# Scores of the first 128 tokens as one unsplit product, from a copy that ScalarE writes

## The chip, the cores and the metric

The kernel runs on one core of a Trainium2 chip. The metric is the device time of one execution in microseconds; the times given are medians of runs. TensorE (PE in the profile) multiplies, VectorE (DVE), ScalarE (ACT) and GpSimd (POOL) work on elements, and SyncE (SP) issues most transfers. Each engine has its own queue and works through it in order; semaphores make one wait for another.

## The reference

Two layers over 512 tokens of width 1024, all in fp32. Each layer has three attention branches with sigmoid gates and an MLP:

```python
for l in range(DEPTH):
    h = _rms_norm(x, attn_norm[l])
    proj = h @ w_in[l]
    ...
    o_a = _dilated_mixture(aq, ak, ...)                 # branch A
    bq = jnp.einsum('bsr,rhe->bshe', _rms_norm(b_ql, ...), w_q_b[l])
    ...                                                 # bk likewise; norms, rotary part
    o_b = _causal_softmax_attention(bq, bk, bv)         # branch B: 8 heads, 96 wide
    o_c = _stick_breaking_attention(c_q, c_k, c_v)      # branch C
    merged = gates[0] * (o_a @ ...) + gates[1] * (o_b @ ...) + gates[2] * (o_c @ ...)
    x = x + merged @ w_out[l]
    h2 = _rms_norm(x, mlp_norm[l])
    x = x + jnp.square(jax.nn.relu(h2 @ w_ff1[l])) @ w_ff2[l]
```

The change is in branch B, for its first block of 128 query tokens (t = 0): `s = q @ k.T * 96**-0.5` under a causal mask, then softmax.

## The kernel before

Activations are kept transposed, 128 rows of the feature axis by 512 tokens. Nearly every product is split: an operand x is held as a high part rounded to float32r and a low part, the rest, and `mm3` (L338 to L340) or `denseA` (L489 to L491) issues high x high, high x low and low x high into one PSUM bank. The splits are made by `split`: ScalarE writes the high part (L346 or L349), VectorE the low part (L347 or L350). Weights are streamed by SP into `raww` and split into `hl` (L250 in the profile, a line that all operations of the weight and gate helpers share).

PSUM has eight banks: three of tag d (psd in the profile, dense products), two of s (pss, scores), two of t (pst, transposes), one of o (pso, outputs). A bank is used again only when its readers are done.

For each head of branch B, `turn` calls `to_qT` for the query and for the key: four transposes on TensorE (L570) bring 512 tokens of the 96-wide head into one bank of tag t, and `split` writes the pair `qT` with the gain column bcol as scale. `score` makes the scores of one block of 128 queries; for t = 0 only 128 keys are needed, but 256 columns are multiplied (m = max(n, 256)). Softmax follows on VectorE (L605) and ScalarE (L608, exponential), `pt_put` transposes the weights (L770, tag t again) and splits them into PP (L346, L347), `causal_out` multiplies with the values. The order within a branch is the hand-written list UNITS_B; `layer` lays it between the dense products of the list ORDER by a credit of estimated times, and a scheduler then fixes the order on each engine.

TensorE's dense products read as streamed operand either tiles of tag a4 (normed activations, trace name a) or of tag u4 (trace name u: the merged branches, read by the output projection, and the squared MLP activations, read by the down-projection). Both are 128 rows by two parts of 512 fp32. In each layer the output projection and each of the four quarters of the down-projection issue 8 tiles x 8 x 3 = 192 products with u.

At the start `warm` writes constants and issues eight products of ones (L378); `kbd_open` fills the unused halves of branch A's key tiles with zeros (L582 on POOL, L583 on VectorE or ScalarE), once in each layer. The tiles of pool kp lie one behind another in the memory, with the other pools behind them; x0, the first one of 2,112 bytes a row, is among the first.

Of the kernel before, what the change touches and what calls it, by code (L numbers as in the profile page):

```python
# [11 lines left out]
AF = mybir.ActivationFunctionType  # L12
# [4 lines left out]
P = 128  # L17
L = 2
D = 1024
S = 512  # L20
# [8 lines left out]
QK = 96  # L29
# [225 lines left out]
class Kern:  # L255
    BUFS = dict(
        raww=2, hl=3, a4=13, x2=9, gt=3, tmp=3, ot=1, sm=8, sm8=4, sm2=4, sm8b=2, u4=16,
        dg=1, raw=2, qT=2, kT=2, SN=9, PT=2, VS=1, PR=2, st=6, mx=8, PP=2, sq=2,
        qT_B=4, SN_B=4, SN_C=3, SR_C=2,
    )  # L260

    PB = dict(d=3, s=2, t=2, o=1)
# [104 lines left out]
    def warm(self, k):  # L367

        nc = self.nc
        self.zero = k([P, 1], "zero")  # L370
        nc.gpsimd.memset(self.zero, 0.0)
        self.ones = k([P, P], "ones")
        nc.vector.memset(self.ones, 1.0)
        self.onesr = k([P, P], "onesr", F32R)
        nc.vector.tensor_copy(self.onesr, self.ones)
        ps = self.ps("o")
        for i in range(self.nwarm):
            nc.tensor.matmul(ps[:, :P], self.ones, self.ones, start=True, stop=True)  # L378

    def setup(self, es):  # L380
        tc, nc = self.tc, self.nc
        self.cp = es.enter_context(tc.tile_pool(name="cp", bufs=1))
        self.kp = es.enter_context(tc.tile_pool(name="kp", bufs=1))
        self.pp = es.enter_context(tc.tile_pool(name="pp", bufs=2, space=PSUM))
        self.wsetup()
        self.x = []
        k = lambda shape, nm, dt=F32: self.kp.tile(shape, dt, name=nm, tag=nm)
        self.bcol = k([96, L, 2], "bcol")
        self.warm(k)
        x0 = k([P, 2 * KT + S], "x0")[:, : KT + S]  # L390
        self.cut = KT + S // 2
        for c in (slice(0, self.cut), slice(self.cut, KT + S)):
            nc.scalar.dma_start(x0[:, c], self.ins["x0g"][:, c])
        nc.scalar.add_instruction(
            mybir.InstLoadActFuncSet(name=nc.get_next_instruction_name(), act_func_set_id=ACT_SET, ins=[], outs=[])
        )
        self.gain0 = x0[:, :KT]
        self.x.append(x0[:, KT:])
        self.wload(1)
        for j in range(1, KT):  # L400
            xt = self.t(self.cp, "x2", [P, S])
            nc.sync.dma_start(xt, self.ins["xT"][j])
            self.x.append(xt)
            if j == 1:
                self.wload(2)
        self.gain = k([P, L, NG], "gain")
        nc.sync.dma_start(self.gain, self.ins["gain"])
        self.ident = k([P, P], "ident")
        self.ropes = k([P, NROPE], "ropes")
        self.masks = k([P, NMASK], "masks", BF16)  # L410
        self.maskA = self.masks[:, C_MA : C_MA + 256]
        self.maskR = self.masks[:, C_MR : C_MR + 256]
        self.maskB = self.masks[:, C_MB : C_MB + 512]
        self.resetC = self.masks[:, C_MC : C_MC + 512]

    def tables(self):

        nc = self.nc
        with self.tc.issue_after(self.wdma[4].ins):
            nc.sync.dma_start(self.ident, self.ins["ident"])  # L420
            nc.sync.dma_start(self.ropes, self.ins["ropes"])
            nc.sync.dma_start(self.masks, self.ins["masks"])
        nc.gpsimd.dma_start(self.bcol, self.ins["bcol"])


    def norm_begin(self, goff, l):
# [135 lines left out]
        nc.gpsimd.tensor_tensor(t, src, grow.unsqueeze(1).to_broadcast([P, 4, 2 * w]), ALU.mult)  # L562
        return t[:, :, 0:w], t[:, :, w : 2 * w]

    def to_qT(self, y, g, d=P):

        nc = self.nc
        ps = self.ps("t")
        for t in range(NT):
            nc.tensor.transpose(ps[:d, t * P : t * P + P], y[:, t], self.ident)  # L570
        hl = self.t(self.tp, "qT", [P, 2, S], F32R)
        self.split(hl[:d, 0], hl[:d, 1], ps[:d], g)
        return hl

    def kbd_open(self):

        nc = self.nc
        z = self.zero.unsqueeze(2)
        self.kbds = []
        for f in (nc.vector.tensor_copy, nc.scalar.copy):  # L580
            k = self.t(self.tp, "kT", [P, 2, 2, S], F32R)
            nc.gpsimd.tensor_copy(k[0:64, :, 1, :], z[0:64].to_broadcast([64, 2, S]))  # L582
            f(k[64:128, :, 0, :], z[64:128].to_broadcast([64, 2, S]))  # L583
            self.kbds.append(k)

    def kbd(self):
# [218 lines left out]
    def layer(self, l):  # L805
# [18 lines left out]
        def thread_A():  # L824
            with tc.tile_pool(name=f"ta{l}", bufs=1) as tp:
                self.tp, self.phase = tp, "A"
                tabs["qn"] = self.rope_tab(R_N, 8, g(21, 53), "tqn")
                tabs["kn"] = self.rope_tab(R_N, 8, g(53, 85), "tkn")
                tabs["qr"] = self.rope_tab(R_R, 8, g(21, 53), "tqr")
                tabs["kr"] = self.rope_tab(R_R, 8, g(53, 85), "tkr")  # L830
                self.kbd_open()
                yield ("open", "A")
                oA = [self.t(self.cp, "a4", [P, 2, S], F32R) for _ in range(2)]
                st["oA"] = oA
                sn, sr, qk, pt, pr, w = {}, {}, {}, {}, {}, {}
                s0 = [self.t(tp, "st", [P, 4, 4]) for _ in range(2)]
                s1 = [self.t(tp, "st", [P, 4, 4]) for _ in range(2)]

                def norm(a, tab):
                    self.head_norm(st[a], 4, HD, 0, 8, tabs[tab])  # L840
                    yield 0.0

                def turn(key, aq, ak, i):
                    pair = lambda a: st[a][:, :, 2 * i : 2 * i + 2].rearrange("p t h d -> p t (h d)")
                    q = self.to_qT(pair(aq), g(19, 20))
                    yield 0.5
                    qk[key] = q, self.to_kbd(pair(ak), g(20, 21))
                    yield 0.5

                def nat(i, t):  # L850
                    self.a_nat(*qk["n", i], i, t, s0[i], sn)
                    yield 0.65

                def res(h, r):
                    self.a_res(*qk["r", h], h, r, s1[h // 2], sr)
                    yield 0.33

                def mix(i):
                    w[i] = self.a_mix(s0[i], s1[i])
                    yield 0.0  # L860

                def scale(h):
                    self.a_scale(h, sn, sr, *w[h // 2])
                    yield 0.0

                def trn(h, half):
                    pt[h, half] = self.a_trn(h, half, sn)
                    yield 0.43

                def trr(h, half):  # L870
                    pr[h, half] = self.a_trr(h, half, sr)
                    yield 0.43

                def out(h):
                    self.a_out(h, [pt[h, 0], pt[h, 1]], [pr[h, 0], pr[h, 1]], st["vA"], st[f"vr{h // 2 + 1}"], oA[h // 2])
                    yield 2.8

                bn = b_norm(0)
                for u in UNITS_A:
                    a = u.split(":")  # L880
                    k, n = a[0], [int(x) for x in a[1:] if x.isdigit()]
                    if k in ("need", "raw"):
                        yield (k, a[1])
                    elif k == "norm":
                        yield from norm(a[1], a[1][0] + ("n" if a[1][1] == "0" else "r"))
                    elif k == "turn":
                        if a[1] == "n":
                            yield from turn(("n", n[0]), "q0", "k0", n[0])
                        else:
                            i = 1 + n[0] // 2  # L890
                            yield from turn(("r", n[0]), f"q{i}", f"k{i}", n[0] % 2)
                    elif k == "bn":
                        yield from bn_part(bn)
                    else:
                        f = dict(nat=nat, res=res, mix=mix, scale=scale, trn=trn, trr=trr, out=out)[k]
                        yield from f(*n)
            yield ("done", "A")
# [7 lines left out]
        def thread_B():  # L905
            with tc.tile_pool(name=f"tb{l}", bufs=1) as tp:
# [6 lines left out]

                def turn(h, name, d, col):
                    def f():
                        d[h] = self.to_qT(st[f"{name}{h // 4}"][:, :, h % 4], self.bcol[:, l, col : col + 1], QK)
                        yield 0.5
                        if name == "bk" and h % 4 == 3:
                            yield ("raw", "bq1" if h == 3 else "cq")
                    return f  # L920

                def score(h, t):
                    def f():
# [2 lines left out]
                        m = max(n, 256)  # L926
                        sl = slice(t * P, t * P + P)
                        q, k = qT[h], kT[h]
                        self.mm3(ps[:, :m], q[:96, 0, sl], q[:96, 1, sl], k[:96, 0, :m], k[:96, 1, :m], True, True)
                        s = self.t(tp, "SN", [P, S])  # L930
                        sm = self.small()
                        self.softmax_scores(ps[:, :n], n, s[:, :n], self.maskB[:, 512 - n :], QK ** -0.5, sm[:, 0:1], sm[:, 1:2])
# [463 lines left out]
```

## Time and profile before

| | us |
|---|---|
| median of 3 runs (1812.24 to 1812.69) | 1812.52 |
| the profiled execution | 1812.14 |
| its span (first to last instruction) | 1810.4 |
| TensorE busy in the span | 1799.3 |
| VectorE busy | 1165.3 |
| ScalarE busy | 931.0 |
| POOL busy | 37.2 |

A row of the timeline gives start, duration, engine, line, operation, out<-in, and in brackets the idle time before it and who ended it; rows of a like kind are merged with their count (x4), and the duration is then that of the whole group. A row of the groups gives line, engine, operation, shapes and count, then busy us and the mean ns of one. Durations of TensorE's products are modelled and overlap, so their spacing is read from start to start. In `128*128 128x512` the first pair is the weight tile (rows * columns), the second the streamed operand.

### The profile page before, as it was taken

How to read it: one execution, taken by the hardware profiler on the slowest of the kernel's cores; microseconds unless marked ns; L12 is line 12 of the kernel's file. 1: busy time of each engine (PE TensorE's matmuls, PEld its weight loads, DVE VectorE, ACT ScalarE, POOL GpSimd, SP SyncE). 2: the span in 40 equal slices, each digit the busy share in tenths (PEclk: the TensorE clock that was granted, in tenths of full speed). 3: DMA queues.
4: the chain of work that ended last, by engine and by line, in shares of the span. 5: the costliest groups of instructions: out<-in, count | busy, mean ns of one | idle time of the engine just before them, and what ended most of it. 6: DMA issues, size and time to landing. Idle time of an engine off the chain costs nothing.

```text
span 1810.4 us, 23064 instructions
## 1 busy us (share of the span) xinstructions
PE 1799.3 (99%) x8592; PEld 1511.7 (84%) x8592; DVE 1165.3 (64%) x2141; ACT 931.0 (51%) x1745; POOL 37.2 (2%) x66
## 2 busy tenths in 40 slices
PE   9999999999999999999999999999999999999999
PEld 8999888878888888888889988887778888888887
DVE  8666899888865343434575568997988653434342
ACT  6646677777734232323355366677877442323241
POOL 1000000000000000000010000000000000000000
PEclk9999999999999999999999999999999999999999
DMA  5222141323353222322432222413234433233332
GB/s 193 87 82 82 59 140 59 117 87 123 123 165 99 97 93 94 104 94 93 137 106 87 82 71 77 145 48 117 80 119 152 145 97 101 93 93 100 98 94 93
DMA packets 64992, 186.79 MB, mean 103 GB/s; under 512 B 11504, under 2 KB 12272, under 8 KB 64880
## 3 DMA queue, kind: packets, MB, share of 16 engines
q1 hardware_dynamic: 57888, 178.57, 30.1%
q0 software_dynamic: 1952, 6.29, 1.0%
q8 instruction: 68, 1.11, 0.2%
q10 hardware_dynamic: 5040, 0.45, 0.2%
q14 instruction: 44, 0.36, 0.1%
HBM read 168.45 MB, written 16.78 MB: 102 GB/s over the span
## 4 chain that ended last, share of the span: by engine, by line
PE 90%; DVE 7%; ACT 3%; issue 1%; DVEq 0%; ACTq 0%
PE psd L491 22%; PE psd L489 22%; PE psd L490 21%; PE psd L338 3%; PE psd L339 3%; PE psd L340 3%; PE pss L338 1%; PE pst L770 1%; DVE SN L987 1%; PE pss L339 1%; PE pss L340 1%; PE pst L570 1%; DVE hl L250 1%; PE pss L979 1%; PE pso L338 1%; PE pso L339 1%
## 5 line engine op out<-in xcount | busy, mean ns | idle before, releaser
L250 ACT CAST hl<-raww 128x1024 fp32r<-128x1024 f32 (+2 forms) x287 | 298.4, 1040 | 664.5 <-PE psd L491 485.1
L489 PE MATMUL psd<-a,hl 128*128 128x512 f32 x1232 | 484.7, 393 | 0.0
L490 PE MATMUL psd<-a,hl 128*128 128x512 f32 x1232 | 483.9, 393 | 0.0
L491 PE MATMUL psd<-a,hl 128*128 128x512 f32 x1232 | 483.6, 393 | 0.0
L250 DVE TENSOR_TENSOR hl<-raww,hl 128x1024 fp32r<-128x1024 f32 (+2 forms) x287 | 347.2, 1211 | 148.2 <-ACT hl L250 147.6
L489 PEld LDWEIGHTS psd<-a,hl 128*128 128x128 f32 x1232 | 231.7, 188 | 44.3
L491 PEld LDWEIGHTS psd<-a,hl 128*128 128x128 f32 x1232 | 231.6, 188 | 44.4
L490 PEld LDWEIGHTS psd<-a,hl 128*128 128x128 f32 x1232 | 231.7, 188 | 44.2 <-issue 0.3
L489 PE MATMUL psd<-u,hl 128*128 128x512 f32 (+1 forms) x648 | 253.6, 391 | 0.0
L491 PE MATMUL psd<-u,hl 128*128 128x512 f32 (+1 forms) x648 | 252.3, 389 | 0.0
L490 PE MATMUL psd<-u,hl 128*128 128x512 f32 (+1 forms) x648 | 249.9, 386 | 0.0
L1328 DVE TENSOR_TENSOR x<-x,psd 128x512 f32<-128x512 f32 x63 | 43.3, 688 | 188.7 <-PE psd L491 188.7
L491 PEld LDWEIGHTS psd<-u,hl 128*128 128x128 f32 x648 | 121.6, 188 | 27.9
L490 PEld LDWEIGHTS psd<-u,hl 128*128 128x128 f32 x648 | 121.6, 188 | 26.5
L1309 DVE SCALAR_TENSOR_TENSOR tmp<-psd,rrep 128x512 f32<-128x512 f32 x64 | 44.3, 692 | 151.9 <-PE psd L491 151.8
L489 PEld LDWEIGHTS psd<-u,hl 128*128 128x128 f32 x648 | 121.9, 188 | 23.7
L338 PE MATMUL psd<-hl,a 128*128 128x512 f32 (+3 forms) x328 | 121.9, 373 | 0.5 <-DVE VS L250 0.5
L339 PE MATMUL psd<-hl,a 128*128 128x512 f32 (+3 forms) x328 | 121.7, 371 | 0.0
L340 PE MATMUL psd<-hl,a 128*128 128x512 f32 (+3 forms) x328 | 121.0, 370 | 0.0
L250 ACT ACTIVATE gt<-gt 128x512 f32<-128x512 f32 x144 | 90.0, 628 | 21.8 <-DVE gt L250 18.5
L338 PEld LDWEIGHTS psd<-hl,a 128*128 128x128 f32 x328 | 79.3, 242 | 4.9 <-DVE VS L250 1.1
L339 PEld LDWEIGHTS psd<-hl,a 128*128 128x128 f32 x328 | 79.2, 241 | 4.1 <-DVE hl L250 0.6
(237 smaller groups left out, 2406.3 us busy)
## 6 DMA issues: line engine op xcount, KB each, us to landing
raww<-w SPq DMA_DIRECT2D x277, 512.0 KB, 3.5
gpark<-gt SPq DMA_DIRECT2D x48, 256.0 KB, 2.4
gt<-gpark SPq DMA_DIRECT2D x48, 256.0 KB, 3.8
x<-xT POOLq DMA_DIRECT2D x8, 256.0 KB, 4.1
park<-x POOLq DMA_DIRECT2D x8, 256.0 KB, 2.3
x<-park POOLq DMA_DIRECT2D x8, 256.0 KB, 3.9
x<-xT SPq DMA_DIRECT2D x7, 256.0 KB, 6.0
outT<-x SPq DMA_DIRECT2D x7, 256.0 KB, 2.0
```

The costliest lines, as they stand in the source:

```text
L250: return f(*a, **k)
L338: mm(ps, ah, bh, start=start, stop=False)
L339: mm(ps, ah, bl, start=False, stop=False)
L340: mm(ps, al, bh, start=False, stop=stop)
L489: self.nc.tensor.matmul(o, w[:, 0, c : c + P], t[:, 0], start=k == 0, stop=False)
L490: self.nc.tensor.matmul(o, w[:, 0, c : c + P], t[:, 1], start=False, stop=False)
L491: self.nc.tensor.matmul(o, w[:, 1, c : c + P], t[:, 0], start=False, stop=k == last)
L570: nc.tensor.transpose(ps[:d, t * P : t * P + P], y[:, t], self.ident)
L770: nc.tensor.transpose(ps[:, kt * P : kt * P + P], s[:, kt * P : kt * P + P], self.ident)
L979: nc.tensor.matmul(ps[:, :m], q[:, hh, sl], k[:, i, hh, :m], start=i == 0, stop=i == 1)
L1309: nc.vector.scalar_tensor_tensor(t, ps, 0.0, self.rrep, ALU.max, ALU.mult)
L1328: nc.vector.tensor_tensor(x, x, ps, ALU.add)
```

## The change

Four edits:

1. `to_qT` gets a further tile `full`: ScalarE writes the first 128 tokens of the transposed head, scaled, unsplit, as plain fp32 (tag q32, four buffers, 128 x 128). It does so for query and key of each head: 32 new instructions.
2. `score` at t = 0 issues one plain fp32 product of 128 columns from these copies in place of the three split ones of 256.
3. x0 is allocated with 4 KT instead of 2 KT extra columns: 2,176 bytes instead of 2,112. All tiles behind it move by 64 bytes. By the built programs the u4 tiles start at byte 152,576 of each partition instead of 152,512 (= 1191.5 x 128), in steps of 4,096; the a4 tiles start at 30,848 (= 241 x 128) in both. qT, kT, PP, SN, ident and masks move as u4 does.
4. The zero fills: POOL fills only the first of the two key tiles, VectorE the lower half of the first and the upper half of the second, ScalarE the rest; in layer 1 they are put behind the copy onesr. The load of bcol goes from POOL's queue to SP's.

```diff
-        qT_B=4, SN_B=4, SN_C=3, SR_C=2,
+        q32=4, qT_B=4, SN_B=4, SN_C=3, SR_C=2,
...
-        nc.vector.tensor_copy(self.onesr, self.ones)
+        onesr = nc.vector.tensor_copy(self.onesr, self.ones)
+        self.kz = lambda: self.tc.issue_after(onesr.ins)
...
-        x0 = k([P, 2 * KT + S], "x0")[:, : KT + S]
+        x0 = k([P, 4 * KT + S], "x0")[:, : KT + S]
...
-        nc.gpsimd.dma_start(self.bcol, self.ins["bcol"])
+        nc.sync.dma_start(self.bcol, self.ins["bcol"])
...
-    def to_qT(self, y, g, d=P):
+    def to_qT(self, y, g, d=P, full=None):
...
         self.split(hl[:d, 0], hl[:d, 1], ps[:d], g)
+        if full is not None:
+            nc.scalar.activation(full[:d], ps[:d, :P], AF.Copy, scale=g)
         return hl
...
-    def kbd_open(self):
+    def kbd_open(self, l):
...
-        for f in (nc.vector.tensor_copy, nc.scalar.copy):
+        for fs in ((nc.gpsimd.tensor_copy, nc.vector.tensor_copy), (nc.vector.tensor_copy, nc.scalar.copy)):
             k = self.t(self.tp, "kT", [P, 2, 2, S], F32R)
-            nc.gpsimd.tensor_copy(k[0:64, :, 1, :], z[0:64].to_broadcast([64, 2, S]))
-            f(k[64:128, :, 0, :], z[64:128].to_broadcast([64, 2, S]))
+            for i, f in enumerate(fs):
+                r = slice(64 * i, 64 * i + 64)
+                with self.kz() if l == 0 else ExitStack():
+                    f(k[r, :, 1 - i, :], z[r].to_broadcast([64, 2, S]))
...
-                        d[h] = self.to_qT(st[f"{name}{h // 4}"][:, :, h % 4], self.bcol[:, l, col : col + 1], QK)
+                        d[h, 0] = self.t(tp, "q32", [P, P])
+                        d[h] = self.to_qT(st[f"{name}{h // 4}"][:, :, h % 4], self.bcol[:, l, col : col + 1], QK, d[h, 0])
...
-                        self.mm3(ps[:, :m], q[:96, 0, sl], q[:96, 1, sl], k[:96, 0, :m], k[:96, 1, :m], True, True)
+                        if t == 0:
+                            nc.tensor.matmul(ps[:, :n], qT[h, 0][:96], kT[h, 0][:96], start=True, stop=True)
+                        else:
+                            self.mm3(ps[:, :m], q[:96, 0, sl], q[:96, 1, sl], k[:96, 0, :m], k[:96, 1, :m], True, True)
```

How the instructions stand on an engine, before and with the change, is shown at two places. The first is TensorE at head 0 of branch B in layer 1. Names are those of the tiles with their numbers: pss are score banks, q_372 and q_369 the new copies of key and query. Before:

```order
L338 MATMUL pss_2102<-qT_2099,qT_2091 128x256
L570 MATMUL pst_2112<-ident,raw_1768 96x128
L338 MATMUL pss_2120<-qT_2099,qT_2091 128x256
L490 MATMUL psd_2319<-a_25_156,hl_2171 128x512
L491 MATMUL psd_2319<-a_25_156,hl_2171 128x512
L489 MATMUL psd_2319<-a_27_162,hl_2171 128x512
L490 MATMUL psd_2319<-a_27_162,hl_2171 128x512
L491 MATMUL psd_2319<-a_27_162,hl_2171 128x512
L339 MATMUL pss_2102<-qT_2099,qT_2091 128x256
L340 MATMUL pss_2102<-qT_2099,qT_2091 128x256
```

With the change, the same engine and place:

```order
L571 MATMUL pst_2115<-ident,raw_1768 96x128 x4
L491 MATMUL psd_2325<-a_27_162,hl_2179 128x512
L492 MATMUL psd_2325<-a_27_162,hl_2179 128x512
L490 MATMUL psd_2325<-a_29_168,hl_2179 128x512
L491 MATMUL psd_2325<-a_29_168,hl_2179 128x512
L492 MATMUL psd_2325<-a_29_168,hl_2179 128x512
L936 MATMUL pss_2106<-q_372_2096,q_369_2086 128x128
L338 MATMUL pss_2124<-qT_2102,qT_2092 128x256
```

The three products into the bank of block 0 (pss_2102 before) have become one (L936), and the scores as a whole have moved behind more dense products.

The second place is the key of head 4 in layer 1, where the bank that the four transposes fill (pst_2779) is taken again two groups of transposes later (pst_2804). ScalarE before, from the split's high part on:

```order
L349 ACTIVATE qT_2773<-pst_2768,bcol 96x512
L346 CAST PP_2078<-pst_2776 128x3x128
L250 ACTIVATE gt_3189<-gt_3189 128x512 x2
L250 CAST hl_3325<-raww_3266 128x1024
L346 CAST PP_2078<-pst_2792 128x4x128
```

ScalarE with the change:

```order
L349 ACTIVATE qT_2784<-pst_2779,bcol 96x512
L346 CAST PP_2078<-pst_2788 128x3x128
L250 ACTIVATE gt_3205<-gt_3205 128x512 x2
L250 CAST hl_3341<-raww_3282 128x1024
L575 ACTIVATE q_532_2778<-pst_2779,bcol 96x128
```

The copy (L575) has come in behind two gate instructions and a weight cast, where before ScalarE was done with that bank after its first row. TensorE with the change, between the two uses of the bank:

```order
L571 MATMUL pst_2779<-ident,raw_2650 96x128 x4
L775 MATMUL pst_2788<-ident,SN_2485 128x128 x3
L490 MATMUL psd_3284<-a_27_162,hl_3065 128x512
...
L490 MATMUL psd_3346<-a_14_124,hl_3175 128x512
L491 MATMUL psd_3346<-a_14_124,hl_3175 128x512
L775 MATMUL pst_2804<-ident,SN_2475 128x128 x4
```

Left out are eight more dense products, so eleven stand between; before there were eight and one score product between the same groups of transposes.

More of the change, by code (lines that the diff above doesn't have):

```diff
@@ L830, in thread_A @@
                 tabs["kr"] = self.rope_tab(R_R, 8, g(53, 85), "tkr")
-                self.kbd_open()
+                self.kbd_open(l)
                 yield ("open", "A")
```

## The prediction

> **What bounds the kernel now.** I read the page first (busy shares and the chain that ended last), then the windows of the stretch in which the second branch runs, then the timeline of TensorE at the lines that change.
>
> ```profile
> span 1810.4 us, 23064 instructions
> PE 1799.3 (99%) x8592; PEld 1511.7 (84%) x8592; DVE 1165.3 (64%) x2141; ACT 931.0 (51%) x1745; POOL 37.2 (2%) x66
> ...
> PE 90%; DVE 7%; ACT 3%; issue 1%; DVEq 0%; ACTq 0%
> ```
>
> TensorE is busy for 99% and carries 90% of the chain. Its ends are modelled, so I go by starts, but the reading stands: what changes TensorE's own time, or makes it wait, arrives at the end; what VectorE and ScalarE do is free until TensorE waits for it. By stretch (columns: PE, PEld, DVE, ACT, POOL busy with counts, granted clock, DMA):
>
> ```profile
> 200.00:330.00 130.00, 129.68 (x729) 109.52 (x728) 121.54 (x303) 97.73 (x216) 6.46 (x9) 1.00 0.26 88
> ...
> 644.00:687.00 43.00, 43.00 (x191) 35.58 (x190) 19.87 (x23) 16.48 (x22) 0.00 (x0) 1.00 0.29 97
> 688.00:731.00 43.00, 43.00 (x190) 35.27 (x189) 15.63 (x17) 9.23 (x10) 0.00 (x0) 1.00 0.30 97
> ```
>
> The first row is the second branch in layer 1: VectorE is busy 121.5 of 130 us and ScalarE 97.7, so little room is left beside TensorE there. The other two are a quarter of the MLP, up- and down-projection, with both helpers mostly idle.
>
> **Part 1, the scores of the first 128 tokens.** Removed: three products of 256 columns for each of 8 heads and 2 layers. Four of them stand in a row here:
>
> ```profile
> 221.91 0.28 PE L339 MATMUL pss<-qT,qT 96*128 96x256 f32 x1
> 222.03 0.28 PE L340 MATMUL pss<-qT,qT 96*128 96x256 f32 x1
> 222.15 0.28 PE L339 MATMUL pss<-qT,qT 96*128 96x256 f32 x1
> 222.26 0.28 PE L340 MATMUL pss<-qT,qT 96*128 96x256 f32 x1
> ```
>
> From start to start (222.26 - 221.91) / 3 = 0.117 us, so three cost 0.35 us. Added: one product of plain fp32 operands, 128 columns. No such product with 96 rows is in the trace, so I bound it by the two kinds of plain fp32 products that are. Both leave two records for each product in the code (the loop at L1090 issues 4 and shows 8, the one at L751 issues 8 or, for two heads together, 16 records for 8).
>
> ```profile
> 1008.46 0.28 PE L340 MATMUL pss<-kT,qT 128*128 128x256 f32 x1
> 1008.57 0.95 PE L1090 MATMUL pso<-ones,tmp 128*128 128x1 f32 x8
> 1009.38 0.37 PE L338 MATMUL pss<-kT,qT 128*128 128x256 f32 x1
> ...
> 157.26 0.28 PE L746 MATMUL pso<-PT,VS 128*128 128x256 f32 x1
> 157.46 1.96 PE L751 MATMUL pso<-PR,x 128*64 128x128 f32 x16
> 159.35 0.38 PE L752 MATMUL pso<-PT,VS 128*128 128x256 f32 x1
> 159.58 0.28 PE L753 MATMUL pso<-PT,VS 128*128 128x256 f32 x1
> ```
>
> At L1090 the end of the split product before is 1008.74 and of the one behind 1009.75: 1.01 us for 8 records and one split product (0.117), 0.11 us a record and nothing for the change of kind. At L751, from L746's start to L753's, 2.32 us hold 16 records and two split products: with (1.96 - 0.27) / 15 = 0.113 us a record and 2 x 0.117, 0.28 us are left over for going in and out. L751 loads only 64 columns of weights (128*64); the new product loads 128 like L1090, so I take L1090: 2 x 0.11 = 0.22 us, a gain of 0.13 each, 16 x 0.13 = **-2.0 us**. The other end, with 0.28 us for each isolated pair: 16 x (0.50 - 0.35) = +2.4 us.
>
> **Part 2, ScalarE's 32 copies, and who waits for them.** The price of one comes from three rows:
>
> ```profile
> L349 ACT ACTIVATE qT<-pst,bcol 96x512 fp32r<-96x512 f32 x32 | 21.8, 680 | 8.3 <-PE pst L570 8.1
> ...
> L346 ACT CAST PP<-pst 128x512 fp32r<-128x512 f32 x32 | 18.6, 580 | 3.9 <-PE pst L770 3.6
> ...
> L346 ACT CAST PP<-pst 128x128 fp32r<-128x128 f32 x32 | 8.5, 264 | 5.0 <-PE pst L770 4.8
> ```
>
> 384 columns fewer are 580 - 264 = 316 ns less, so the scaled copy of 128 columns is about 680 - 316 = 0.36 us; 32 of them are 11.6 us of ScalarE. The copy is no matter for its length, but it reads the transposed tile in PSUM, tag t with two banks. The transposes after the next must wait until it is done, and on ScalarE it stands behind other work. This is the second place shown in the section on the change (the key of head 4), as it ran before:
>
> ```profile
> 278.05 0.61 PE L570 MATMUL pst<-ident,raw 128*96 128x128 f32 x4
> 278.50 0.49 PE L770 MATMUL pst<-ident,SN 128*128 128x128 f32 x3
> 278.70 0.69 ACT L349 ACTIVATE qT<-pst,bcol 96x512 fp32r<-96x512 f32 x1 [1.98 <-PE pst L570]
> ...
> 279.29 0.46 ACT L346 CAST PP<-pst 128x384 fp32r<-128x384 f32 x1
> ...
> 279.65 1.30 ACT L250 ACTIVATE gt<-gt 128x512 f32<-128x512 f32 x2
> 279.89 0.74 DVE L350 SCALAR_TENSOR_TENSOR qT<-pst,bcol,qT 96x512 fp32r<-96x512 f32 x1
> ...
> 280.86 1.03 ACT L250 CAST hl<-raww 128x1024 fp32r<-128x1024 f32 x1
> ...
> 281.06 0.60 PE L770 MATMUL pst<-ident,SN 128*128 128x128 f32 x4
> ```
>
> The bank that L570 filled at 278.05 is taken again by the four transposes at 281.06. Before, VectorE's L350 released it at 280.63 and nobody waited. Now the copy stands behind two sigmoids and a weight cast, so it runs from about 281.85 to 282.2. In the new order three transposes and eleven split products stand between, 3 x 0.11 + 11 x 0.23 = 2.9 us from 278.50, so TensorE arrives at 281.35 and waits about 0.9 us; in both layers 1.8 us. At the other turns I compared the same two sums by the order and these durations: four of the remaining fifteen per layer come out within 0.3 us of each other, the rest leave a microsecond or more. I add 0.5 us for those: **+2.3 us**, between 0 (ScalarE catches up elsewhere) and ten such stalls, 9 us. The new product itself also waits for both copies, but 2.5 to 20 us of other products stand between. VectorE's queue only gains from what is removed: nothing.
>
> **Part 3, the padding.** It moves every tile behind it by 64 bytes: u4 (the trace's u) from byte 152,512, which is 64 over a multiple of 128, to 152,576, which is a multiple; the a4 tiles (the trace's a) have the same shape and lie on a multiple in both. Both stream 512 columns against the same hl weights in blocks of 8 x 24 = 192 products (three lines, 64 each):
>
> ```profile
> 643.90 0.40 PE L489 MATMUL psd<-a,hl 128*128 128x512 f32 x1
> ...
> 687.47 0.40 PE L489 MATMUL psd<-u,hl 128*128 128x512 f32 x1
> ...
> 731.43 0.40 PE L489 MATMUL psd<-a,hl 128*128 128x512 f32 x1
> ...
> L489 PE MATMUL psd<-a,hl 128*128 128x512 f32 x64 | 24.9, 390 | 0.0
> ...
> L489 PE MATMUL psd<-u,hl 128*128 128x512 f32 x64 | 25.2, 394 | 0.0
> ```
>
> With a, 687.47 - 643.90 = 43.57 us; with u, 731.43 - 687.47 = 43.96 us, though the helpers do less there (windows above). There are four such blocks of u and one of the output projection in each layer: 10 x 0.39 = **-3.9 us** if the start address is the reason. The other end is 0. The same shift reaches about 180 products of 512 columns whose streamed tile lies behind u4's offset (qT, kT, PP): at the same 2 ns each 180 x 2 ns = **-0.4 us**, between 0 and -1.
>
> **Part 4, the head and the zero fills.** One of POOL's fills goes to VectorE, behind onesr, and the bcol load goes from POOL's queue to SP's, ahead of a weight load.
>
> ```profile
> 1.75 2.31 DVE L375 CAST onesr<-ones 128x128 fp32r<-128x128 f32 x1
> 4.18 0.36 DVE L439 TENSOR_SCALAR a<-x 128x256 fp32r<-128x256 f32 x1
> ...
> 4.03 0.62 ACT L250 CAST hl<-raww 128x512 fp32r<-128x512 f32 x1
> ...
> 4.70 1.22 PE L338 MATMUL psd<-hl,a 128*128 128x512 f32 x2
> ...
> 25.42 0.92 ACT L250 CAST hl<-raww 128x864 fp32r<-128x864 f32 x1 [2.94 <-DMA raww<-w]
> ...
> 34.05 0.29 PE L338 MATMUL psd<-hl,a 128*128 128x288 f32 x1
> ```
>
> VectorE's fills end earlier or later by some tenths, but the first product starts at 4.70 with ScalarE's cast (4.03 + 0.62), which nothing moves: 0, at most +-0.4. In front of layer 2 the fill that POOL loses is one more short instruction for VectorE in a stretch like the third window, where it is busy 15.63 of 43 us: 0. The loads behind bcol come one issue later, under half a microsecond; the weights cast at 25.42 are first used at 34.05: covered.
>
> **The order.** The scheduler also puts other rows of the second branch in another order; TensorE's sum of products stays, and I set 0, +-1 us.
>
> **Sum.** -2.0 + 2.3 - 3.9 - 0.4 = -4.0 us. The profiled execution took 1812.14 us (span 1810.4), 0.4 below the median of 1812.52; I carry the difference to the median: **1808.5 us**. 0.2%, about what a measurement can tell from no change, is 3.6 us, so this stands just beyond that bound.
>
> **Rivals.**
> *The address is not the reason.* For it speaks that u and a differ in more than the offset: u lies higher in the memory, and no tile of the trace has the one without the other. Against it: the shapes, the weights and the loop are the same, and the helpers, which could disturb the reading, do less while u is read. Then 1812.52 - 2.0 + 2.3 = 1812.8 us. The Trainium skill, "SBUF — State Buffer", Specifications (TRN2), gives lines of 16 bytes and a penalty for each line crossed; 64 bytes are a whole number of such lines, so by that rule the padding would change nothing, and the two blocks above should be equal, which they are not.
> *The new product pays for going in and out as L751 does*: +2.4 instead of -2.0, so 1812.9 us, and 1817 us without part 3.
> *The copies hold the PSUM banks (slower).* Seven of the sixteen turns in a layer have a weight cast (1.03 us above) between the split and the copy. If all fourteen stall as at 281.06, 14 x 0.9 = 12.6 us instead of 2.3: 1818.8 us. Slower by 0.2% it becomes from 10 us on, eleven stalls of 32 turns. Against it: most turns have more products between than this one.
> *The waits don't appear*: 1806.2 us.
>
> **Chances.** All parts as summed: 0.50 (1806.5 to 1811; three fifths of it beyond 0.2%). Without the waits, or with more from the addresses: 0.16, faster. Address no reason: 0.20, within 0.2%. In and out like L751: 0.06, within but for a third. Copies hold the banks: 0.08, three quarters of it slower. Faster by 0.2%: 0.30 + 0.16 = 0.46; slower 0.02 + 0.06 = 0.08; the rest 0.46. The range of 1805.5 to 1813.5 us takes in the first case, its neighbours and the case without part 3.
>
> **What would show it.** A block of u in 43.57 us instead of 43.96; two records 0.11 us apart for each new product, with the split product behind it on time; a wait of TensorE for ScalarE's copy once or twice a layer, near 281 us and at the like place of layer 2; the first product still at 4.7 us. The forecast is wrong if u stays at 43.96 us, if gaps of 0.3 us surround the new products, or if waits for the copy stand at more than ten turns.

## The result: 12 us slower

| | median, us | ratio to before, 95% interval |
|---|---|---|
| before | 1812.55 | |
| changed | 1824.80 | 1.0069 (1.0057 to 1.0080) |

The forecast was 1808.5 us, in a range of 1805.5 to 1813.5. The page of the changed kernel, its span and TensorE:

```profile
span 1823.5 us, 23025 instructions
...
PE 1809.5 (99%) x8576; PEld 1509.3 (83%) x8576; DVE 1164.7 (64%) x2143; ACT 938.3 (51%) x1777; POOL 34.7 (2%) x63
```

TensorE has fewer products and is busy 10 us longer. The timeline of the changed kernel at the starts of the blocks of 192 dense products (layer 1, MLP) tells where:

```profile
603.84 0.40 PE L490 MATMUL psd<-u,hl 128*128 128x512 f32 x1
...
648.63 0.39 PE L490 MATMUL psd<-a,hl 128*128 128x512 f32 x1
...
692.17 0.40 PE L490 MATMUL psd<-u,hl 128*128 128x512 f32 x1
...
736.96 0.39 PE L490 MATMUL psd<-a,hl 128*128 128x512 f32 x1
```

A block of a is nearly as before (692.17 - 648.63 = 43.54 us, against 43.57). A block of u takes 44.79 us, not the 43.57 forecast and not the 43.96 of before: 0.83 more each, **8.3 us for the ten blocks**. Inside one, the products of the changed kernel start alternately 0.23 and 0.24 us apart and nothing waits:

```profile
699.86 0.39 PE L490 MATMUL psd<-u,hl 128*128 128x512 f32 x1
700.09 0.40 PE L491 MATMUL psd<-u,hl 128*128 128x512 f32 x1
700.33 0.39 PE L492 MATMUL psd<-u,hl 128*128 128x512 f32 x1
700.56 0.40 PE L490 MATMUL psd<-u,hl 128*128 128x512 f32 x1
700.80 0.39 PE L491 MATMUL psd<-u,hl 128*128 128x512 f32 x1
```

A block over its 192 products is 233.3 ns a product for u, against 229.0 before, and 226.7 to 226.9 for a in both. The rest of the loss lies in the second branch: by the starts of the dense products, counted one by one, TensorE falls back by a further 2.3 us in each layer there.

### The profile page after: what moved, and what is told of

Read it like the earlier page. It is cut to its first block, busy times and chain, and to the rows that moved or that the text cites. A ratio compares the mean times of both kernels' runs of the same rounds, so it can differ in the third digit from the quotient of the medians.

```text
span 1823.5 us, 23025 instructions
## 1 busy us (share of the span) xinstructions
PE 1809.5 (99%) x8576; PEld 1509.3 (83%) x8576; DVE 1164.7 (64%) x2143; ACT 938.3 (51%) x1777; POOL 34.7 (2%) x63
## 4 chain that ended last, share of the span: by engine, by line
PE 88%; DVE 7%; ACT 3%; issue 1%; DMA 0%; ACTq 0%; DVEq 0%
PE psd L492 21%; PE psd L491 21%; PE psd L490 21%; PE psd L339 3%; PE psd L338 3%; PE psd L340 3%; DVE SN L996 2%; PE pst L775 1%; PE pss L338 1%; PE pss L340 1%; PE pss L339 1%; PE pst L571 1%; DVE hl L250 1%; PE pss L988 1%; PE pso L339 1%; PE pso L338 1%
```

## The experiments

Addresses below are start addresses in a partition, by the built programs.

### The padding alone, both ways

```diff
# in the changed kernel            (e1)
-        x0 = k([P, 4 * KT + S], "x0")
+        x0 = k([P, 2 * KT + S], "x0")
# in the kernel before             (e2; e3 with 8 * KT)
-        x0 = k([P, 2 * KT + S], "x0")
+        x0 = k([P, 4 * KT + S], "x0")
```

> The changed kernel with the padding behind x0 as it was (2 x 64 bytes instead of 4 x 64 counted as bytes of the tile's tail: x0 2*KT+S again), all else as changed. Theory A (the tile u4's start address sets the pace of its products): the u blocks go back from 44.8 to 43.96 us, 10 x 0.83 = 8.3 us less, 1816.5 us, still 4 us above the kernel before. Theory B (the padding has no part in it; scores, copies and fills make the loss): 1824.8 us, u blocks still 44.8 us.

> The kernel before with the padding alone (x0 4*KT+S, u4 from byte 152,576). Theory A (start address): u's products every 233 ns instead of 229, 10 blocks x 192 products x 4.3 ns = +8.3 us, 1820.8 us. Theory B (the other edits slow the u blocks, for example by other work beside them): 1812.5 us and 229 ns.

> The kernel before with 192 bytes more instead of 64 behind x0 (x0 8*KT+S): u4 from byte 152,704, which is 128 over a multiple of 512, as the fast a4 tiles and the weight tiles hl are. Theory A1 (the pace goes by the start address modulo 512 or 256): u's products every 226.7 ns like a's, 10 x 192 x -2.25 ns = -4.3 us, 1808.2 us. Theory A2 (only a multiple of 128 matters, and it is the slow case): 233 ns and 1820.8 us. Theory A3 (anything but the 64 of before is noise of another cause): 229 ns, 1812.5 us.

Measured: e1 1816.82 us (1.0022; 1.0013 to 1.0031), e2 1821.37 (1.0046; 1.0033 to 1.0058), e3 1808.38 (0.9976; 0.9967 to 0.9985). Taken out of the change the padding gives back 8.0 us, put into the kernel before it costs 8.8: it is two thirds of the loss. With 192 bytes in place of 64, the kernel is 4.2 us faster than before and the fastest kernel here. The timeline of e3:

```profile
643.39 0.39 PE L489 MATMUL psd<-a,hl 128*128 128x512 f32 x1
...
686.91 0.39 PE L489 MATMUL psd<-u,hl 128*128 128x512 f32 x1
...
730.43 0.39 PE L489 MATMUL psd<-a,hl 128*128 128x512 f32 x1
```

a and u now take the same 43.52 us. e2 and e3 differ from the kernel before in addresses alone, so theory B is out. A2 (a multiple of 128 is the slow case) is out too: 152,704 is one.

### Its own address, or its distance from the weights

e4 spreads the addresses within one run; e9 moves all three kinds of tiles together; e10 tries another distance.

```diff
# e4
-            hl = self.t(self.cp, "hl", [P, 2, 1024], F32R)
+            hl = self.t(self.cp, "hl", [P, 2 * 1024 + 16], F32R)[:, :2048].rearrange(...)
-                ut = self.t(self.fp, "u4", [P, 2, S], F32R)
+                ut = self.ut()     # [P, 2 * S + 8], the first 2 * S of it
# e9                                                  (and x0 with 8 * KT)
-            t = self.t(self.cp, "raww", [P, 1024])
+            t = self.t(self.cp, "raww", [P, 1024 + 16])
# e10
-        x0 = k([P, 2 * KT + S], "x0")
+        x0 = k([P, 16 * KT + S], "x0")
```

> The kernel before with each of the 16 u4 tiles 32 bytes longer (so 16 start addresses, 32 bytes apart modulo 512) and each of the 3 weight tiles hl 64 bytes longer (3 start addresses of the weights). Read is the spacing of products by u tile and hl tile. Theory A1 (streamed tile's own start address modulo 256 or 512): the spacing goes up and down with the u tile, between about 226.5 and 233 ns, the same for each hl tile. Theory A1r (address relative to the weights): the pattern shifts by 64 or 128 bytes from one hl tile to the next. Theory B: one spacing, 229 ns, for all tiles. The time of the whole is then somewhere between 1808 and 1821 us.

> The kernel before with everything from the second weight-load buffer on moved by 128 bytes and u4 by 192 more, so that the a4, hl and u4 tiles all start 256 over a multiple of 512 (before: a4 and hl at 128, u4 at 448). Theory R (what counts is the streamed tile's start relative to the weights', modulo 512 or a divisor of it): all at one class, 226.7 ns for a and u, 1808.4 us. Theory D (absolute: 128 over a multiple of 512 is a good place and others are not): a's products slow too, 3,700 of them by 2 to 6 ns, 1820 to 1840 us.

> The kernel before with 448 bytes more behind x0: u4 at 384 over a multiple of 512, so 256 from the weights' class. If the classes repeat every 256 bytes: 226.7 ns for u, about 1808.4 us. If they repeat every 512 only: between 229 and 234 ns, 1812 to 1822 us.

e4 took 1832.85 us (one run), more than any theory gave, since a's products became slow as well. Its timeline in a block of a, at each change of the weight tile (24 products; the tiles start, in this order, at 128, 256, 192 and 128 over a multiple of 512):

```profile
655.29 0.39 PE L493 MATMUL psd<-a,hl 128*128 128x512 f32 x1
...
660.77 0.40 PE L493 MATMUL psd<-a,hl 128*128 128x512 f32 x1
...
666.36 0.39 PE L493 MATMUL psd<-a,hl 128*128 128x512 f32 x1
...
671.96 0.39 PE L493 MATMUL psd<-a,hl 128*128 128x512 f32 x1
...
677.41 0.40 PE L493 MATMUL psd<-a,hl 128*128 128x512 f32 x1
```

The same streamed tiles, at 128 over, take 5.48, 5.59, 5.60 and 5.45 us: with the weights at their own class 227 to 228 ns a product, with the weights 64 or 128 bytes further 233. So for a it is the distance between the two that counts. u's products in e4 did not show the shifting pattern that A1r expected: their streamed tile, and with it the distance, changes at every third product, and the means by address lie between 231 and 234 ns. Those at distance 0 took 231.2 ns on average and not 226.7, so the distance of a product to its own weights is not all that counts once products at other distances stand beside it. The reason stays open.

e9, with all three at 256 over, took 1808.59 us (0.9978; 0.9969 to 0.9988): 128 over is no good place of its own, theory D is out. e10 took 1809.31 us (one run):

```profile
687.73 0.39 PE L489 MATMUL psd<-u,hl 128*128 128x512 f32 x1
...
731.25 0.39 PE L489 MATMUL psd<-a,hl 128*128 128x512 f32 x1
```

43.52 us again at a distance of 256 over a multiple of 512, the same as at 0. Spacing by the distance (streamed tile less weights, modulo 256), where all neighbouring products have the same one:

| distance | ns | from |
|---|---|---|
| 0 | 226.7 to 226.9 | a in all but e4; u in e3, e9, e10, e13 |
| 64 | 229.0 | u before |
| 128 | 233.3; 232.9 | u changed and in e2; a with the second weight tile in e4 |
| 192 | 233.3 | a with the third weight tile in e4 |

Modulo 512 the three slow distances were 320, 384 and 448; that 64, 128 and 192 themselves give the same is assumed and was not tried.

TensorE loads the next weights while it streams (PEld is busy for 83% of the span beside TensorE's 99%), so both reads are under way at once; that they disturb each other fits, but the runs show the distance and not the mechanism. The Trainium skill, "TensorE: Matmul & The Clock Gate", Step-by-step: what each phase is for, has the two reads on independent ports, and says that loading the next weights "doesn't steal SBUF read bandwidth from the running matmul". By that the distance would not matter; here it moves the spacing by 3%, and the measurement decides.

### The zero fills alone

```diff
# the diff's part 4 in the kernel before: kz, kbd_open(l), bcol on SP's queue
```

> The kernel before with part 4 alone: one of POOL's two zero fills of each layer goes to VectorE, the fills of layer 1 are put behind onesr, and the load of bcol goes to SP's queue. Theory H (the head pays for it): the head of the changed kernel lost 0.9 to 1.3 us by the count of products, so 1813.4 to 1813.8 us, with the second half of the first weight block waited for to about 5.5 us instead of 4.99. Rival N (the head is costed at nothing, and what was lost there came from the other edits): 1812.5 us, weight half waited to 4.99.

1812.41 us (1.0001; 0.9993 to 1.0010): nothing, as part 4 had it. By the hundredth dense product the profile of the changed kernel had lost 1.4 us (38.99 against 37.62). Its rows, and then those of e13, which has the same head:

```profile
4.70 1.22 PE L338 MATMUL psd<-hl,a 128*128 128x512 f32 x2
5.54 0.62 ACT L250 CAST hl<-raww 128x512 fp32r<-128x512 f32 x1 [0.90 <-DMA raww<-w]
```

```profile
4.89 1.20 PE L338 MATMUL psd<-hl,a 128*128 128x512 f32 x2
5.18 0.62 ACT L250 CAST hl<-raww 128x512 fp32r<-128x512 f32 x1 [0.36 <-DMA raww<-w]
```

In one profiled execution a transfer landed 0.36 us later than in the other, and e13 has its hundredth product at 37.54. The late landing is not the whole of the 1.4 us, and the rest stays open; but since e5 and e13 have the same fills and don't lose it, it is no effect of the fills.

### Copies and products, together and apart

```diff
# e6: the diff's q32, full and score, no padding, no fills
# e7: q32 and full alone (score as before)
# e8: score alone
+                            nc.tensor.matmul(ps[:, :n], q[:96, 0, :P].bitcast(F32), k[:96, 0, :P].bitcast(F32), ...)
```

> The kernel before with parts 1 and 2 alone: the 32 copies of ScalarE and the 16 plain products, padding and fills as before. Theory S (copies and products make 2.2 us of loss in each layer's second branch): 1812.5 + 4.4 - 1 (head) = about 1816 us. Rival F (the fills shift the schedule of the second branch and make most of it): 1812.5 to 1813.5 us.

> The kernel before with the 32 copies of ScalarE alone; nothing reads them, the three split products stay. Theory S: the copies' waits without the product's gain, 2.0 us more than both together, about 1818 us. Rival W (the waits belong to the product's new order, not to the copies): 1812.5 to 1814 us.

> The kernel before with the 16 plain products alone, which read the high parts of the split tiles as plain fp32; the low parts of the first 128 tokens' scores are left out, and no copies run. If the product costs 0.22 us instead of 0.35: -2.0 us, 1810.5 us. If it pays for going in and out of its kind as the product at L751 does: +2.4 us, 1814.9 us.

e6 1817.19 us (1.0026; 1.0015 to 1.0037), e7 1815.80 (1.0019; 1.0010 to 1.0028), e8 1812.67 (1.0002; 0.9993 to 1.0011). Together they cost +4.9 us, of which the copies alone are +3.5. That is theory S in its direction, but not in its order: it had e7 2.0 us above e6, and e7 lies 1.4 us below. The product alone gains nothing that can be measured, and beside the copies it makes things worse. Two places of e8 between split products, and one behind transposes:

```profile
279.27 0.40 PE L490 MATMUL psd<-a,hl 128*128 128x512 f32 x1
279.65 0.49 PE L930 MATMUL pss<-qT,qT 96*128 96x128 f32 x2
279.89 0.48 PE L491 MATMUL psd<-a,hl 128*128 128x512 f32 x1
280.22 0.40 PE L489 MATMUL psd<-a,hl 128*128 128x512 f32 x1
...
279.65 0.30 PEld L930 LDWEIGHTS pss<-qT,qT 96*128 96x128 f32 x2 [0.41 <-ACT qT L349]
```

```profile
230.18 0.39 PE L489 MATMUL psd<-a,hl 128*128 128x512 f32 x1
230.41 0.38 PE L930 MATMUL pss<-qT,qT 96*128 96x128 f32 x2
230.55 0.48 PE L490 MATMUL psd<-a,hl 128*128 128x512 f32 x1
230.86 0.40 PE L491 MATMUL psd<-a,hl 128*128 128x512 f32 x1
...
302.64 0.39 PE L930 MATMUL pss<-qT,qT 96*128 96x128 f32 x2
302.79 0.42 PE L338 MATMUL pss<-qT,qT 96*128 96x384 f32 x1
303.04 0.34 PE L339 MATMUL pss<-qT,qT 96*128 96x384 f32 x1
```

At the first place, 0.95 us from 279.27 to 280.22 hold two split products (0.227 each) and the new one: 0.50 us. But its weight load had waited for ScalarE's high part (L349), 0.41 us. At the second the neighbours are split products as well, its weight load stood idle for 0.07 us only, and 0.68 us from 230.18 to 230.86 leave 0.23 for it. Behind transposes, which are plain fp32 like it, 0.40 us from 302.64 to 303.04 hold it and one product of 384 columns (0.18): 0.22 us. So no charge for the change of kind can be seen. What goes with a higher price is a weight load that comes late: in the changed kernel twelve of the sixteen cost 0.22 to 0.24 us, and the four at 0.36 to 0.38 are those whose weight load stood idle for 0.3 us before it, two for a copy (L575) and two for VectorE (L610). In e8 the two costliest of each layer are the one above and one at 308.62, whose load stood idle for 0.2 us with nothing in the profile to say why. The mean of the sixteen, worked out in this way, is 0.29 us in e8 and 0.26 in the changed kernel: -0.9 and -1.4 us.

### What the copies cost

```diff
# e11: in e7, the copy reads the split tile
-            nc.scalar.activation(full[:d], ps[:d, :P], AF.Copy, scale=g)
+            nc.scalar.activation(full[:d], hl[:d, 0, :P].bitcast(F32), AF.Copy)
# e14: in e11, a second such copy of the next 128 columns
# e12: in e6, with x0 of e3, the copy ahead of the split
+            if full is not None:
+                nc.scalar.activation(full[:d], ps[:d, :P], AF.Copy, scale=g)
         self.split(hl[:d, 0], hl[:d, 1], ps[:d], g)
```

> The kernel before with 32 copies on ScalarE as in the run of the copies alone, but read from the high part of the split tile and not from the transposed tile in PSUM; nothing reads them. Theory B (the copies cost time because they hold the PSUM bank for the next transposes): 1812.5 to 1813 us. Rival L (they cost time because ScalarE is nearly full beside the second branch, whatever they read): about 1815.8 us, as the run of the copies alone.

> The kernel before with 64 copies on ScalarE, all read from the high part of the split tile, two for each tile; nothing reads them. With 32 such copies it was 1.7 us slower than before, with an interval that reaches to zero. Theory L (ScalarE's load beside the second branch costs time by itself): about twice that, 1816 us or more, since 9.8 us more of ScalarE stand in the same 2 x 130 us. Rival Q (what the 32 cost came from a chance order of the rows): 1812.5 to 1814.5 us.

> The kernel before with the padding of 192 bytes, the 16 plain products and the copies, but each copy issued ahead of the split of its tile, so that no other work stands between them on ScalarE. Theory B (the bank held behind other ScalarE work): the release comes 0.36 us later than before and not 2 us, so the waits shrink from 3.5 to about 1 us: 1808.4 + 1 - 0.9 (products at 0.29 us) = about 1808.5 us. Rival L (ScalarE's load): 1808.4 + 4.9 = 1813.3 us.

e11 1814.28 us (1.0007; 0.9998 to 1.0015), e14 1813.79 (1.0009; 1.0000 to 1.0017), e12 1812.31 (0.9998; 0.9989 to 1.0007). Twice the load costs no more than once, which speaks against ScalarE's load. e11 lies between its two theories: by the medians 1.8 to 2.1 of the 3.5 us need the read of PSUM, though the intervals of e7 and e11 overlap. The profile of e7 has the same size: those who waited for its copies (us, times) are

```profile
  PEld pst L772: 1.1, 4
  PEld pst L570: 0.7, 2
```

In e6, where the product is there too and the order is another, twelve such waits take 4.1 us, which is the likely reason why e6 is slower than e7.

What the other 1.4 to 1.7 us are (their intervals reach to nothing) stays open: a different order of the rows could be it, but that was not tried by itself. With the copy ahead, e12 is 3.9 us above e3, which has the same padding, in place of e6's 4.9: issuing it earlier helps by one microsecond and not by the four and more that theory B gave. The split, and with it the bank's release, still comes a copy later; whether that is the whole of the rest was not tried.

The copies in the changed kernel, first from its groups, then who waited for them (us, times):

```profile
L575 ACT ACTIVATE q<-pst,bcol 96x128 f32<-96x128 f32 x32 | 11.6, 361 | 5.6 <-DVE qT L350 5.2
```

```profile
  PEld pst L571: 2.4, 6
  PEld pst L775: 1.2, 4
  PEld pss L936: 0.6, 2
```

361 ns each, as estimated. But the releaser is VectorE's low part (L350): where the copy had nothing else ahead of it, it started only when that was done, though it needs nothing from it. Both read one PSUM bank. The Trainium skill, "PSUM — Partial Sum Buffer", PSUM bank collisions raise a hardware error, says that the compiler's scheduler adds a dependency between two engines that touch one bank in the same 32 partitions, reads included; the row agrees. So wherever the copy comes behind L350, the bank is held for a copy longer. The place that the prediction singled out, in the changed kernel:

```profile
279.65 0.60 PE L571 MATMUL pst<-ident,raw 128*96 128x128 f32 x4
...
280.29 0.69 ACT L349 ACTIVATE qT<-pst,bcol 96x512 fp32r<-96x512 f32 x1 [1.97 <-PE pst L571]
...
281.46 0.74 DVE L350 SCALAR_TENSOR_TENSOR qT<-pst,bcol,qT 96x512 fp32r<-96x512 f32 x1
...
282.44 1.03 ACT L250 CAST hl<-raww 128x1024 fp32r<-128x1024 f32 x1
...
282.93 0.60 PE L775 MATMUL pst<-ident,SN 128*128 128x128 f32 x4
...
283.37 0.36 ACT L575 ACTIVATE q<-pst,bcol 96x128 f32<-96x128 f32 x1
...
283.78 0.39 PEld L571 LDWEIGHTS pst<-ident,raw 128*96 128x96 f32 x4 [0.34 <-ACT q L575]
```

The copy does stand behind the weight cast, 1.17 us after L350 ended. But the transposes at 282.93 began before it, since they had the other bank: by the built program pst_2779 lies in bank 7, and pst_2788 and pst_2804 both in bank 6. So the section on the change is wrong where it says that pst_2804 takes the bank of pst_2779 again; in the kernel before, the groups at the same places did share one. Bank 7 goes to the next group of transposes (283.78), which waited for the copy, 0.34 us and not 0.9. There are ten such waits of transposes and two of the product, 4.2 us by the rows above.

### The change with the other padding

```diff
# in the changed kernel
-        x0 = k([P, 4 * KT + S], "x0")
+        x0 = k([P, 8 * KT + S], "x0")
```

> The changed kernel with 192 more bytes behind x0 instead of 64, so that u4 starts a multiple of 256 from the weights hl. Theory R (start relative to the weights, modulo 256) with the other terms as the single edits showed them: 1824.8 - 10 x 192 x (233.3 - 226.7) ns = 1824.8 - 12.7 = 1812.1 us. Rival I (the scores' loss grows when u is fast, because the terms don't add): 1813.5 us and more.

1812.20 us (1.0000; 0.9991 to 1.0010): 12.6 us less than the changed kernel, 12.7 expected. So the padding's term adds to the others. Beside the kernel before it would have passed for "no change", with a gain of 4.2 us and a loss of about 4 inside.

## Why the prediction was wrong, step by step

- **Part 3, the padding (-3.9 us): the step that failed, by its sign.** That the start address sets the pace was right, and worth more than thought: it measured +8.0 to +8.8 us. The wrong step was to compare the addresses with a round number (u4 comes to a multiple of 128, as a4 is one), while what counts is the distance from hl, 0 for a, 64 before, 128 with the change. With two tiles and two addresses the trace of before could not tell these apart, and so a loss had to stand among the ends; "the other end is 0" left it out, and with it the sign of the whole. The rival "the address is not the reason" was wrong as well: 64 bytes moved the spacing by 4.3 ns. The -0.4 us for the other shifted products can't be told from nothing: e2's 8.8 us leave 0.5 beyond the ten blocks, within its interval.
- **Part 2, the waits (+2.3 us): right in kind, too small.** With -1.4 us for the products, e1's +4.3 leaves 5.7 us for waits and order; e7 measured 3.5 for the copies alone. At the one place costed, the transposes named had the other bank, and the next group waited 0.34 us where 0.9 was set. Left out was that a copy waits for L350 too. Transposes waited at five places in each layer, 0.21 to 0.48 us each, 3.6 us in all, where one long wait and a little at four others, 2.3 us, were counted; the product's own wait for a copy, 0.6 us, was set at nothing. The slower rival (fourteen stalls of 0.9 us) named the mechanism, with a price too high.
- **Part 1, the product (-2.0 us): right in kind, a little too large.** The 0.22 us held for twelve of the sixteen, and L1090 was the right nearest row: L751's 0.28 us for going in and out does not appear between split products. The other four paid for a late weight load, so -1.4 us came of it (-0.9 in e8).
- **Part 4 and the first product at 4.7 us** held: 0.1 us.
- **Order (0 +-1 us)**: e8 loses again the 0.9 us that its products gain, so by the medians order was worth about +1.2 us there (0.35 + 0.9), with an interval wider than that.

Sum by the single edits: +8.0 to +8.8 (padding), +4.9 (copies and products), +0.1 (fills), 13.0 to 13.8 against 12.3 measured, which is within the intervals.

## What to carry to other kernels

Where two operands are read at once, look at their start addresses relative to each other and not at round numbers, and try the padding that makes the class equal: one line, 4.2 us here. When a trace shows two speeds for the same work at two addresses, a third address can be slower than both, so price an address change with both signs. A short read of a shared PSUM bank is priced by when the bank comes free. Before the price of a product is put down to its kind, read what its weight load waited for. One change can hold a gain and a loss that cancel, so measure its edits apart.

## What the runs showed of the hardware

- Products of 512 columns that stream from SBUF while the next weights load start every 226.7 to 226.9 ns when both tiles lie at the same place modulo 256 bytes, every 229.0 ns at 64 bytes of distance and every 233 ns at 128 and 192, as long as the neighbouring products have the same distance (in e4, where they don't, 231 to 234 ns at every one).
- A plain fp32 product of 128 columns costs 0.22 to 0.24 us both between split products and behind other plain ones (transposes), and 0.29 to 0.50 where its weight load stood idle for 0.2 us and more before it.
